# Windowed attention of the odd layer: one pinned plan over 64 head groups, wider value products, the output norm in two steps

## The chip, the cores and the metric

The kernel runs on one core of a Trainium2 chip. The metric is device time in microseconds (us), the median over the runs shown. TensorE is PE in the profile (its weight loads PEld), VectorE is DVE, ScalarE is ACT, GpSimd is POOL, SyncE is SP. Sums are made in one profiled execution.

## The reference, cut to what matters

Two layers over 2048 latent tokens of width 1024 and 256 context tokens. Layer 0 (Fourier mixing beside latent attention) is not touched. Layer 1 is windowed attention with 16 query heads in 4 key/value groups of 4 heads (dimension 64): a block of 128 queries sees the 256 context keys and the three blocks of keys around it, under a mask of +-128 tokens, with one sink logit per head. Its gated output goes through `w_out`, is added to the stream, and a final RMSNorm is stored.

```python
q, k, v, g = split_cols(h_lat @ w_in, ODD_SPLITS)
q, k = apply_rope(q, *rope), apply_rope(k, *rope)
y_l = (windowed_gqa(q, k, v, ck, cv, sink) * silu(g)) @ w_out   # softmax over [ctx, band, sink]
x = x + g_l * y_l
return rmsnorm(x, final_g)
```

## The kernel before, in words

Precision is kept by splitting a float32 operand into a high and a low part; `mm3` (L185 to L188) multiplies two such pairs in three products (high*high, high*low, low*high), so each output product stands under L186, L187 and L188.

**Projection of layer 1** (loop over `seq`, L1688 on). Three passes over the chunks of tokens (1,2,3 / 4,5,6,0 / 7,8), each over five column blocks of `w_in`: 0 and 1 are queries, 2 keys and values, 3 and 4 the gate. In the third pass the order is gate, gate, queries, queries, keys/values (`p2o`). A rotated block is finished in `finish_t` (L1666): VectorE multiplies by the tables, POOL adds, ScalarE rounds the high half, POOL makes the low half; the four stores of the two halves go out one item later (`pend`, `flush`). In the last columns of the third pass the first loads and the row maxima of attention block 0 are mixed in (lists `e6`): all four head groups of block 0, its `chain` and its first `aug`.

**Attention** (L1805 on). 16 query blocks x 4 groups = 64 head groups, each over 4 or 5 key tiles, 312 steps in all. One step (`step6`) is on TensorE a mask product where the tile is at the edge of the band (L1813), two score products of 512 columns (L1814, L1815), then on ScalarE two exponentials (float32 L1819, float16 L1820), and a subtraction that gives the low float16 part (L1821, mostly POOL). `pv` then multiplies probabilities by values: for each of 4 heads a product of 65, of 64 and of 65 columns (L1831 to L1833, the first two with the same weights), into a one-bank accumulator of which there are two. After the last tile of a group VectorE adds the sink term, inverts and scales (L1837 to L1840), and POOL multiplies the gate (L1842).

The exponent is shifted by each row's maximum. `max_band` (L1525 on TensorE, L1529 on VectorE) and `max_ctx` (L1538, L1541) find it from the rounded queries `Q1`; `chain(b)` (L1544 to L1562) joins the maxima of a whole block of 16 heads, splits the result into a high and a low part, and `aug` (L1566 transpose, L1567 copy) puts it into eight extra rows of `Q2`, under the second score product.

Around it: `out_tr` (L1868) transposes the gated rows of the block before into one accumulator bank (`ppo`, one buffer), `split` (L180, L183) writes them to SBUF, `out_mm` multiplies by `w_out` (16 x `mm3`), VectorE and POOL add to the stream (L1882, L1883), and `out_fin` squares, takes the root and scales (L1889 to L1894) and stores. `load_q6` brings the queries of a group in three DMAs (L150). `wload` and `wsplit` bring and split `w_out` during block 0 and 1, through two raw buffers (`wr6`).

What sets the order: a list `plan` per block, with positions as fractions of the block from tables in `TP`. The steps of the next block stand there (`load_q6`, the maxima, `chain` at 0.94, `aug` of its first group at 0.96, the products of the block before). `pv` runs four steps behind the scores. SP's DMAs are kept in program order; TensorE's instructions are not in this part (`pe = nc.tensor` at L1270): the compiler's scheduler may place them otherwise. `pe_ordered` (L152) pins them.

Of the kernel before, what the change touches and what calls it, by code (L numbers as in the profile page):

```python
# [65 lines left out]
class Pool:  # L66
# [36 lines left out]
    'p2o': [3, 4, 0, 1, 2],  # L103
    'b0': {'mx': [0.1, 0.41, 0.59, 0.68], 'mcd': [0.1, 0.26, 0.08, 0.13]},
    'wa': 6,
    'wb': 15,
    'wp': [0.02, 0.0],
    'wd': [0.9, 0.5],
    'we': [0, 0, 0, 0, 0, 0, 0, 0, 0, 0, 0, 0, 0, 0, 0, 1],
    'pps': 3,  # L110
    'ppv': 2,
    'ppo': 1,
    'ppx': 2,
    'pf': 4,
# [27 lines left out]
def tile_hybrid(ctx: ExitStack, tc: tile.TileContext, A, out, dumps=None, stop=99):  # L142
# [1304 lines left out]
    c6, qp6, qs6, sm6, pp6, yp6 = sbuf(), sbuf(), sbuf(), sbuf(2), sbuf(6), sbuf()  # L1447
    wr6 = sbuf(2)
    C6, KL, V1, KV, KK = {}, {}, {}, {}, {}

    def const6():
        C6["mb"] = c6.tile([P, 384], F32, name="mb")
        sp.dma_start(C6["mb"], A["c_band"])
        C6["mask8"] = c6.tile([8, 4, P], F32, name="mask8b")
        sp.dma_start(C6["mask8"], A["c_mask8"])
        sk8 = C6["sk8"] = c6.tile([P, 16], F32, name="sk8")
        sp.dma_start(sk8, A["o_sink"].to_broadcast([P, 16]))
        dve.tensor_scalar(sk8, sk8, 1.0 / GQA_SCALE, None, op0=ALU.mult)
# [16 lines left out]
    def prep_k(t):  # L1475
# [4 lines left out]
        def p0():  # L1480
# [35 lines left out]
    def max_band(b, kv, j):  # L1516
# [3 lines left out]
        if b not in MX:  # L1520
            MX[b] = sm6.tile([P, 2, 16], F32, tag="mx", name=f"mx6_{b}")
# [23 lines left out]
    def chain(b):  # L1545
# [12 lines left out]
        if b:  # L1558
            sink(b)
# [585 lines left out]
```

## Time and profile before

| what | us |
|---|---|
| median of 3 runs | 3030.02 (3030.01 to 3030.97) |
| profiled execution, its own time | 3034.24 |
| its span, first to last instruction | 3032.2 |
| PE busy in the span | 2861.0 (94%) |
| PEld, POOL, DVE, ACT busy | 2299.7, 1632.0, 1462.6, 1427.4 |

Matmuls are pipelined, and a row's duration is longer than the distance to the next start; where a cost of TensorE is wanted, distances between starts are read. The attention of layer 1 begins near 2335 us in the span. PEclk in a table is the granted TensorE clock as a share of 2.4 GHz, averaged over two levels (2.4 and 1.2 GHz).

### The profile page before, as it was taken

The numbers are of one execution on the slowest core, as the hardware profiler recorded it, in microseconds if no ns is written. First come the engines' busy times: TensorE is split into PE (matmuls) and PEld (weight loads), VectorE is DVE, ScalarE is ACT, GpSimd is POOL, SyncE is SP. The second block draws the span as 40 slices with busy tenths as digits, with TensorE's granted clock in tenths as the row PEclk, the third lists the DMA queues.
The fourth block names the chain that finished last, engine by engine and source line by source line (L and its number), as shares of the span: only waits on it lengthen the run. The fifth ranks groups of instructions, "written<-read, shape, count | busy, mean of one in ns | idle before, by whom it ended". The sixth has DMA issues, their size and how long they took to land. (4 is left out here: it accounts for less than half of the span.)

```text
span 3032.2 us, 54284 instructions
## 1 busy us (share of the span) xinstructions
PE 2861.0 (94%) x21388; PEld 2299.7 (76%) x21388; DVE 1462.6 (48%) x2884; ACT 1427.4 (47%) x2131; POOL 1632.0 (54%) x1221
## 2 busy tenths in 40 slices
PE   7999999999999999999999998999997899999998
PEld 4787777877777777777777888989786666677666
DVE  3323315453656665666542234323234666676664
ACT  4333213223577777777773332232222645554554
POOL 2202204035588888888784434353443766766665
PEclk9999999999999999999999998999998999999999
DMA  6453335466310111011016545544464333223321
GB/s 240 153 177 134 130 122 173 142 213 223 104 44 26 44 40 44 26 44 40 26 35 232 188 153 177 187 141 162 152 189 156 105 105 98 84 77 93 102 83 45
DMA packets 299399, 357.13 MB, mean 118 GB/s; under 512 B 40884, under 2 KB 210172, under 8 KB 299144
## 3 DMA queue, kind: packets, MB, share of 16 engines
q1 hardware_dynamic: 231320, 258.73, 27.0%
q10 hardware_dynamic: 67824, 94.93, 8.9%
q8 instruction: 168, 2.75, 0.4%
q14 instruction: 87, 0.71, 0.1%
HBM read 245.82 MB, written 107.76 MB: 117 GB/s over the span
## 5 line engine op out<-in xcount | busy, mean ns | idle before, releaser
L186 PE MATMUL psb<-sbr 128*128 128x512 f32 (+3 forms) x2054 | 744.3, 363 | 14.4 <-ACT sbf L1022 5.7
L188 PE MATMUL psb<-sbr 128*128 128x512 f32 (+3 forms) x2054 | 722.9, 352 | 4.8 <-DVE sbr L183 4.8
L187 PE MATMUL psb<-sbr 128*128 128x512 f32 (+3 forms) x2054 | 723.8, 352 | 2.2 <-POOL sbr L183 2.2
L1188 POOL TENSOR_TENSOR sbf<-sbf 128x1024 f16<-128x1024 f32 (+1 forms) x296 | 624.2, 2112 | 140.8 <-ACT sbf L1187 76.9
L155 PE MATMUL psb<-sbr 100*128 100x512 f32 (+1 forms) x2408 | 624.2, 399 | 21.0 <-DVE sbr L955 14.4
L155 PEld LDWEIGHTS psb<-sbr 100*128 100x128 f32 (+1 forms) x2408 | 425.0, 190 | 112.8 <-issue 17.3
L942 DVE TENSOR_REDUCE sbf<-psb 128x1 f32<-128x512 f32 (+1 forms) x584 | 400.7, 690 | 218.1 <-PE psb L155 203.5
L186 PEld LDWEIGHTS psb<-sbr 128*128 128x128 f32 (+1 forms) x2054 | 390.7, 190 | 81.0 <-issue 12.3
L188 PEld LDWEIGHTS psb<-sbr 128*128 128x128 f32 (+1 forms) x2054 | 390.2, 190 | 63.9 <-DVE sbr L183 6.8
L187 PEld LDWEIGHTS psb<-sbr 128*128 128x128 f32 (+1 forms) x2054 | 390.8, 190 | 53.2 <-POOL sbr L183 3.9
L1821 POOL TENSOR_TENSOR sbf<-sbf 128x512 f16<-128x512 f32 x282 | 338.0, 1213 | 116.0 <-issue 60.1
L1186 ACT ACTIVATE sbf<-psb 128x1024 f32<-128x1024 f32 (+1 forms) x296 | 299.6, 1012 | 200.4 <-PE psb L155 180.5
L183 DVE TENSOR_TENSOR sbr<-sbf,sbr 128x512 fp32r<-128x512 f32 (+3 forms) x212 | 209.1, 1014 | 382.2 <-ACT sbr L180 381.1
L180 ACT CAST sbr<-sbf 128x512 fp32r<-128x512 f32 (+4 forms) x286 | 198.2, 731 | 394.5 <-PE psb L187 149.5
L183 POOL TENSOR_TENSOR sbr<-sbf,sbr 128x512 fp32r<-128x512 f32 (+4 forms) x113 | 166.1, 1482 | 367.9 <-ACT sbr L180 226.3
L1819 ACT ACTIVATE sbf<-psb 128x512 f32<-128x512 f32 x312 | 188.4, 604 | 282.1 <-PE psb L1815 249.8
L1187 ACT ACTIVATE sbf<-psb 128x1024 f16<-128x1024 f32 (+1 forms) x296 | 297.8, 1006 | 0.0
L155 PEld LDWEIGHTS <-sbf 128*128 128x128 f16 x4672 | 213.5, 97 | 72.9 <-issue 65.9
L155 PE MATMUL psb<-sbf 128*128 128x129 f16 (+1 forms) x4672 | 256.8, 207 | 5.2 <-DVE sbf L1214 2.9
L1529 DVE CUSTOM_DVE_ANT_0 sbf<-psb,sbf 128x384 bf16<-128x384 f32 (+1 forms) x256 | 137.8, 538 | 119.4 <-PE psb L1525 108.1
L1820 ACT ACTIVATE sbf<-psb 128x512 f16<-128x512 f32 x312 | 188.2, 603 | 5.5 <-DMA vd<-sbf 5.5
L1831 PEld LDWEIGHTS <-sbf 128*128 128x128 f16 x1248 | 115.5, 97 | 68.3 <-issue 61.8
(259 smaller groups left out, 4303.9 us busy)
## 6 DMA issues: line engine op xcount, KB each, us to landing
sbf<-in_o_w_in_t SPq DMA_DIRECT2D x60, 512.0 KB
sbf<-in_w_in_t SPq DMA_DIRECT2D x54, 512.0 KB
sbf<-in_x SPq DMA_DIRECT2D x32, 512.0 KB
sbf<-in_w_mod SPq DMA_DIRECT2D x32, 512.0 KB
sbr<-q1h SPq DMA_DIRECT2D x128, 128.0 KB
h1d<-sbf ACTq DMA_DIRECT2D x9, 1024.0 KB
sbf<-h1d SPq DMA_DIRECT2D x18, 512.0 KB
x1d<-sbf ACTq DMA_DIRECT2D x16, 512.0 KB
```

The costliest lines, as they stand in the source:

```text
L155: tc.keep_in_program_order(nc.tensor.matmul(*args, **kw))
L180: act.copy(hi, src)
L183: e_lo.tensor_sub(lo, src, hi)
L186: pe.matmul(ps, sh, mh, start=start, stop=False)
L187: pe.matmul(ps, sh, ml, start=False, stop=False)
L188: pe.matmul(ps, sl, mh, start=False, stop=stop)
L942: dve.reduce_max(st["mx"][:, js[0] : js[-1] + 1, c], ps[:, 0 : len(js) * kn].rearrange("p (j k) -> p j k", k=kn), axis=AX.X)
L1186: act.activation(pf[:, :, 0:n], ps[:, :, 0:n], AF.Exp, scale=MLA_SCALE)
L1187: act.activation(ph[:, :, 0:n], ps[:, :, 0:n], AF.Exp, scale=MLA_SCALE)
L1188: pool.tensor_sub(pl[:, :, 0:n], pf[:, :, 0:n], ph[:, :, 0:n])
L1819: act.activation(pf, ps, AF.Exp, scale=GQA_SCALE)
L1821: (dve if (TP["b0"].get("sub", TP["sub"]) if b == 0 else TP["sub"])[kv][n] else pool).tensor_sub(pl, pf, ph)
```

## The change

One plan for all 64 groups with positions counted in steps; TensorE pinned to program order in the attention; steps in pairs (two scores, then two value products six steps behind); the exponent's shift per group instead of per block, in one rounded part; the two products with the same weights joined into one of 129 columns, in an accumulator of two banks, of which there is one; the low part subtracted for two steps at once, on POOL; the output norm split (`out_fin`, `out_end`). In the projection the gate blocks go last in pass three, rotated blocks are rounded and halved one item on and stored one further on, and the gate's stores go out one item on; only two groups of block 0 have their maxima there. `w_out` has three raw buffers.

```diff
-    'p2o': [3, 4, 0, 1, 2],
+    'p2o': [0, 1, 2, 3, 4],
...
-    wr6 = sbuf(2)
+    wr6 = sbuf(3)
...
-    def chain(b):
...
-        dve.tensor_max(m, mx[:, 0, :], mx[:, 1, :])
-        dve.tensor_max(m, m, sk8)
-        dve.tensor_scalar(m, m, -1.0, SHIFT / GQA_SCALE, op0=ALU.mult, op1=ALU.add)
...
-        dve.tensor_copy(m8[:, :, 0, :].bitcast(F32R), m4)
-        dve.tensor_sub(m8[:, :, 1, :].bitcast(F32R), m4, m8[:, :, 0, :])
...
-        pool.tensor_add(es, m, sk8)
...
+    def chain(b, kv):
+
+        m = sm6.tile([P, 4], F32, tag="m", name=f"m6_{b}_{kv}")
+        dve.reduce_max(m, C6["mx", 4 * (b % 2) + kv], axis=AX.X)
+        v = VM[b, kv] = sm6.tile([P, 4], F32, tag="vm", name=f"vm6_{b}_{kv}", bufs=3)
+        act.activation(v.bitcast(F32R), m, AF.Copy, bias=SHIFT / GQA_SCALE, scale=-1.0)
+        es = ES[b, kv] = sm6.tile([P, 4], F32, tag="es", name=f"es6_{b}_{kv}", bufs=4)
+        pool.tensor_add(es, v, C6["sk8"][:, 4 * kv : 4 * kv + 4])
...
-        [lambda: load_q6(0, 0)] + [nop] * 5 + max_all(0),
-        [lambda kv=kv: load_q6(0, kv) for kv in range(1, 4)] + [nop] * 3 + max_all(1) + max_all(2) + max_all(3)
-        + [lambda: chain(0)] + [nop] * 3 + [lambda: aug(0, 0)],
...
+        [nop] * 4 + [const6_end, lambda: load_q6(0, 0)] + [nop] * 4,
+        [nop] * 4 + max_all(0) + [lambda: chain(0, 0)],
+        [lambda: load_q6(0, 1), lambda: load_q6(0, 2), *pk[4]] + [nop] * 4 + max_all(1) + [lambda: chain(0, 1), nop]
+        + [lambda: aug(0, 0)],
...
+        def halve():
+            rh, rl = halves()
             act.copy(rh.bitcast(F32R), r)
             pool.tensor_sub(rl.bitcast(F32R), r, rh)
...
+            pend.append(lambda: store_t(rh, rl, i, rows))
+
+        pend.append(halve)
...
+                flush()
+                pend.append(lambda d=g1d[2 * i + j - 2][:, hf * 512 : (hf + 1) * 512], e=e: act.dma_start(d, e))
...
-    pps, ppv, ppo = psum(TP['pps']), psum(TP['ppv']), psum(TP['ppo'])
+    pe = pe_ordered
+    pps, ppv, ppo = psum(3), psum(1), psum(1)
...
+        if not x:
+            PF["f"] = pp6.tile([P, 2, 512], F32, tag="pf", name=f"pf6_{b}_{kv}_{t}", bufs=2)
...
+        if b == 15 and kv == 3 and n > 1:
+            (pool if x else dve).tensor_sub(pl, pf[:, x], ph)
+        elif x:
+            pool.tensor_sub(PF["l"], pf, PF["h"])
...
+                O[b, kv] = ppv.tile([P, 1024], F32, tag="o", name=f"o6_{b}_{kv}")
...
-                pe.matmul(o, ph[:, js], v[:, kv, 0:65], start=n == 0 and j == 0, stop=False)
-                pe.matmul(o[:, 0:64], ph[:, js], v[:, kv, 65:129], start=False, stop=False)
-                pe.matmul(o, pl[:, js], v[:, kv, 0:65], start=False, stop=last and j == 3)
+                if j % 2 and n:
+                    pe.matmul(o[:, 0:65], pl[:, js], v[:, kv, 0:65], start=False, stop=False)
+                    pe.matmul(o, ph[:, js], v[:, kv, 0:129], start=False, stop=last)
+                else:
+                    pe.matmul(o, ph[:, js], v[:, kv, 0:129], start=n == 0 and j % 2 == 0, stop=False)
+                    pe.matmul(o[:, 0:65], pl[:, js], v[:, kv, 0:65], start=False, stop=last and j % 2 == 1)
...
+                for j in range(4):
+                    dve.scalar_tensor_tensor(t1[:, j], p4[:, j, 65:129], den[:, j], t1[:, j], op0=ALU.mult, op1=ALU.add)
...
-                (dve if b == 15 and kv == 3 else pool).tensor_mul(g, g, t1)
...
+                pool.tensor_mul(g, g, t1)
...
-        dve.tensor_scalar(v, ss, 1.0 / D, EPS, op0=ALU.mult, op1=ALU.add)
+        act.activation(v, ss, AF.Copy, bias=EPS, scale=1.0 / D)
         rsqrt(y, v)
-        dve.scalar_tensor_tensor(x, x, y, C6["fgb"], op0=ALU.mult, op1=ALU.mult)
+        pool.tensor_mul(x, x, C6["fgb"])
+        YS[b] = x, y
+
+    def out_end(b):
+        x, y = YS.pop(b)
+        act.mul(x, x, y)
         sp.dma_start(out[b * P : (b + 1) * P, :], x)
...
+    for u, (b, kv) in enumerate(groups):
+        if u > 2:
+            at(start[u - 5] + 0.3 if u > 5 else -1, lambda b=b, kv=kv: load_q6(b, kv))
+        if u > 1:
+            s0 = start[u] - 9
+            for j in range(4):
+                at(s0 + 0.8 * j, lambda b=b, kv=kv, j=j: max_band(b, kv, j))
+            for jj in range(2):
+                at(s0 + 3.2 + 0.8 * jj, lambda b=b, kv=kv, jj=jj: max_ctx(b, kv, jj))
+            at(s0 + 4.1, lambda b=b, kv=kv: (chain(b, kv), sink(b, kv)))
+        if u:
+            at(start[u] - 2.2, lambda b=b, kv=kv: aug(b, kv))
+    for x in range(TP["wa"], 17):
+        w0 = 1.5 * (x - TP["wa"] - 1) if x > TP["wa"] else -1
...
+        t0, t1, m0, md = (8.2, 10.2, 13.8, 0.85) if b < 13 else (8.2, 10.2, 12.8, 0.42) if b == 13 else (3, 6, 6.5, 0.42)
+        at(s1 + t0, lambda b=b: out_tr(b, 0))
+        at(s1 + t1, lambda b=b: out_tr(b, 1))
+        at(s1 + m0, lambda b=b: out_load(b))
+        for i in range(16):
+            at(s1 + m0 + md * i, lambda b=b, i=i: out_mm(b, i // 8, i % 8))
+        at(s1 + m0 + md * 16 + 0.6, lambda b=b: out_fin(b))
+        at(s1 + m0 + md * 16 + (4.5 if b < 14 else 1.0), lambda b=b: out_end(b))
...
+                turn = g % 2 == 0 and len(pvq) > 5 and pvq[0][1]
+                if turn:
+                    pvq.pop(0)[0]()
+                    late = 1
+                step6(b, kv, n, t, nts[b], g % 2)
+                g += 1
+                run(min(g - 0.5, S[15] + 14.9))
+                if g % 2 == 0:
+                    run_pv((6 if b < 15 else 4) + late)
+                    late = 0
+                    run(min(g, S[15] + 14.9))
```

## Rows read from the trace of the kernel before

**Rows 1.** Windows: busy us (count) of PE, PEld, DVE, ACT, POOL; clock, DMA, GB/s.
```profile
2282.00:2335.00 53.00, 42.25 (x315) 41.89 (x316) 27.22 (x67) 9.95 (x17) 20.67 (x21) 0.87 0.46 146
2335.00:2384.50 49.50, 33.11 (x278) 22.79 (x276) 26.42 (x65) 26.13 (x50) 36.84 (x35) 0.76 0.48 149
2432.70:2947.50 514.80, 476.28 (x4562) 357.05 (x4560) 342.58 (x828) 277.53 (x542) 336.80 (x313) 0.99 0.31 89
```

**Rows 2.** Waits of PE, 2384.5 to 2947.5: total us, times, longest.
```profile
PE psb L1525 <- DMA sbr<-q1l: 14.2, 8, 2.2
PE psb L1566 <- DVE sbf L1555: 9.7, 13, 0.8
PE psb L1868 <- DVE sby L183: 8.7, 13, 0.7
PE psb L1525 <- DMA sbr<-q1h: 5.3, 4, 1.9
```

**Rows 3.** Waits of SP's queue, 2370 to 3010: total us, times, longest.
```profile
SPq L150 <- DVE sbf L1894: 356.4, 14, 25.6
```

**Rows 4.** Timeline of PE in block 1: start, duration, line, shape, idle before.
```profile
2417.62 0.48 PE L1814 MATMUL psb<-sbr 128*128 128x512 f32 x1
2417.94 0.40 PE L1815 MATMUL psb<-sbr 72*128 72x512 f32 x1
2418.18 0.21 PE L1831 MATMUL psb<-sbf 128*128 128x65 f16 x1
...
2418.56 0.38 PE L1813 MATMUL psb<-sbf 128*128 128x512 bf16 x1
...
2419.00 0.39 PE L1815 MATMUL psb<-sbr 72*128 72x512 f32 x1
2420.13 0.27 PE L1566 MATMUL psb<-sbf 128*8 128x128 f32 x1 [0.74 <-DVE sbf L1555]
```

**Rows 5.** Timeline of PE at the end of block 1.
```profile
2428.89 0.19 PE L1833 MATMUL psb<-sbf 128*128 128x65 f16 x1
2429.75 0.66 PE L1868 MATMUL psb<-sbf 128*128 128x128 f32 x4 [0.67 <-DVE sby L183]
...
2435.21 0.58 PE L1525 MATMUL psb<-sbr 128*128 128x384 f32 x2 [2.21 <-DMA sbr<-q1l]
```

**Rows 6.** Windows of two whole blocks, columns as in rows 1.
```profile
2564.40:2608.27 43.87, 40.27 (x380) 30.64 (x380) 28.58 (x69) 22.84 (x46) 27.80 (x26) 0.96 0.34 89
2649.97:2692.33 42.36, 39.29 (x381) 29.24 (x380) 28.55 (x69) 23.15 (x46) 28.06 (x27) 1.00 0.31 93
```

**Rows 7.** Timeline of PE in layer 0's attention: 16 products, 8 of 129 columns, 8 of 65.
```profile
1004.69 0.87 PE L155 MATMUL psb<-sbf 128*128 128x129 f16 x16
1005.36 2.10 PE L155 MATMUL psb<-sbr 100*128 100x512 f32 x8
```

**Rows 8.** Waits of PE, 2282 to 2384.5.
```profile
PE psb L1525 <- DMA sbr<-q1l: 12.6, 4, 6.2
PE psb L1525 <- DVE sbf L1529: 7.8, 2, 7.4
```

**Rows 9.** The page's group of POOL's pair subtraction in layer 0's attention.
```profile
L1188 POOL TENSOR_TENSOR sbf<-sbf 128x1024 f16<-128x1024 f32 (+1 forms) x296 | 624.2, 2112 | 140.8 <-ACT sbf L1187 76.9
```

**Rows 10.** Groups of POOL and DVE, 2334 to 3032: busy us, mean ns | idle before.
```profile
L1821 POOL TENSOR_TENSOR sbf<-sbf 128x512 f16<-128x512 f32 x282 | 338.0, 1213 | 116.0 <-issue 60.1 <-ACT sbf L1820 37.1 <-POOL sbf L1821 12.2
L1842 POOL TENSOR_TENSOR sbf<-sbf 128x256 f32<-128x256 f32 x63 | 52.0, 825 | 103.1 <-DVE sbf L1840 91.4 <-PE psb L1538 11.7
L1883 POOL TENSOR_TENSOR sbf<-sbf 128x512 f32<-128x512 f32 x30 | 38.5, 1282 | 2.1 <-DVE sbf L1882 1.6
L183 POOL TENSOR_TENSOR sbr<-sbf,sbr 128x512 fp32r<-128x512 f32 x10 | 13.2, 1317 | 3.1 <-ACT sbr L180 3.0
L1840 DVE TENSOR_TENSOR sbf<-psb,sbf 128x256 f32<-128x256 f32 x64 | 27.1, 424 | 2.3
L1837 DVE TENSOR_TENSOR sbf<-psb,sbf 128x4 f32<-128x4 f32 x64 | 10.2, 160 | 9.8 <-PE psb L1833 8.0
```

More of the change, by code (lines that the diff above doesn't have):

```diff
@@ L1657, in flush @@
     def flush():
-        while pend:
+        for _ in range(len(pend)):
             pend.pop(0)()
@@ L1668, in finish_t, with halves @@
         pv = ps.rearrange("p (f t) -> p f t", f=2)
[L1669 to L1670 removed]
+        def halves():
+            return [ep5.tile([P, 2, 256], F32, tag=t, name=f"{t}5_{n}_{i}", bufs=2) for t in ("rh", "rl")]
         if i:
@@ L1900, in tail_tr @@
     def tail_tr(q, k0, n):
+        if not q:
+            YT[15] = (
+                yp6.tile([P, KT, P], F32R, tag="yh", name="yh6_15"),
+                yp6.tile([P, KT, P], F32R, tag="yl", name="yl6_15"),
+            )
         yh, yl = YT[15]
@@ L1952, in tail_end, with tiles_of, at @@
             (sp if hf else act).dma_start(out[15 * P : 16 * P, hsl], x[:, hsl])
-    parity = 0
-    for b in range(16 - TP["nb"], 16):
+    def tiles_of(b):
+        lo, hi = band(b)
+        return [0, 1] + [2 + i for i in range(lo, hi + 1)]
+    nts = [len(tiles_of(b)) for b in range(16)]
+    S = [4 * sum(nts[:b]) for b in range(17)]
+    groups = [(b, kv) for b in range(16) for kv in range(4)]
+    start = [S[b] + kv * nts[b] for b, kv in groups]
+    plan = []
+    def at(pos, f):
+        plan.append((pos, len(plan), f))
@@ L1956, in tile_hybrid, with g_load @@
+    def g_load(b):
         G[b] = yp6.tile([P, D], F32, tag="g", name=f"g6_{b}", bufs=2)
         sp.dma_start(G[b], g1d[b])
[L1958 to L1978 removed]
@@ L1995, in tile_hybrid @@
-        if b == 15:
-            at(TP["z"][11], lambda: out_fin(14))
-            for kv in range(1, 4):
-                at(TP["z"][11 + kv], lambda kv=kv: aug(15, kv))
-        elif b:
-            at(T["ofin"], lambda: out_fin(b - 1))
-        if b < 15:
-            for f in prep_k(b + 5):
-                at(0.1, f)
-            for kv in range(4):
-                at(T["ql"][kv], lambda kv=kv: load_q6(b + 1, kv))
-                m0 = T["mx"][kv]
-                for j in range(4):
-                    at(m0 + T["mxd"][kv] * j / 4, lambda kv=kv, j=j: max_band(b + 1, kv, j))
-                for jj in range(2):
-                    at(T["mc"][kv] + T["mcd"][kv] * jj, lambda kv=kv, jj=jj: max_ctx(b + 1, kv, jj))
-            at(T["ch"], lambda: chain(b + 1))
-            at(T["aug0"], lambda: aug(b + 1, 0))
@@ new lines, in tile_hybrid, with run, run_pv @@
+    at(S[15] + 14.5, lambda: out_load(15))
+    at(S[15] + 13.4, lambda: tail_tr(0, 0, 4))
+    for i in range(8):
+        at(S[15] + 15 + 0.1 * i, lambda i=i: tail_mm(i // 2, i % 2))
+    plan.sort(key=lambda z: z[:2])
+    def run(pos):
+        while plan and plan[0][0] < pos:
+            plan.pop(0)[2]()
+    def run_pv(keep):
+        while len(pvq) > keep:
+            pvq.pop(0)[0]()
+    run(0)
+    g = late = 0
+    for b in range(16):
+        for kv in range(4):
+            for n, t in enumerate(tiles_of(b)):
+                turn = g % 2 == 0 and len(pvq) > 5 and pvq[0][1]
+                if turn:
+                    pvq.pop(0)[0]()
+                    late = 1
[6 more added lines that the diff above has]
+                    run(min(g, S[15] + 14.9))
@@ L2035, in tile_hybrid @@
+    tail_tr(1, 4, 2)
+    run(S[15] + 15.45)
+    run_pv(2)
+    run(S[16])
+    tail_mm(4, 0)
+    run_pv(0)
+    tail_mm(4, 1)
+    tail_mm(5, 0)
+    tail_mm(5, 1)
+    tail_tr(2, 6, 2)
     tail_end()
```

226 lines of the change are left out of this document (68 added, 158 removed).

## The prediction

> **What bounds the kernel now.** I read the windows first. In the long stretch of like blocks, 2432.7 to 2947.5, PE is busy 476.3 of 514.8 us at a clock of 0.99, POOL 336.8, DVE 342.6, ACT 277.5 [rows 1]: TensorE bounds it, and what an edit is worth is the TensorE time that it frees. Before that stretch lies the join of projection and attention, 2282 to 2384.5: 102.5 us of which PE is busy 75.4, at clocks of 0.87 and 0.76 [rows 1]; there other things bound.
>
> Then the waits of PE in the blocks [rows 2]. Three stand out, each about once per block: `max_band` for query loads (14.2 + 5.3 us), `aug` for the `chain` (9.7), and the second `out_tr` for the halving of the first (8.7). The queue of SP says where the loads were: 356.4 us in 14 waits for L1894, the last step of the output norm [rows 3]. The store stands in SP's order ahead of the next block's loads. The timelines show the size of each: L1815 at 2419.00 to L1566 at 2420.13 is 1.13 us where the same product is followed after 0.24 at 2417.94 to 2418.18 [rows 4]; L1833 to L1868 takes 0.86 [rows 5] where products of that width are about 0.03 apart (twelve in 0.38, 2418.18 to 2418.56 [rows 4]). The wait for the load there is 2.21 [rows 5].
>
> **The change part by part.**
>
> *Query loads.* `load_q6` issues three DMAs on SP. They now come five groups ahead of their group's scores and about 16 steps (some 30 us at 42.36 us per 20 steps [rows 6]) ahead of its maxima, so a store that holds SP for some us delays nothing that PE needs. The store itself (`out_end`) stands 3.9 steps behind `out_fin`, and the next `out_load`, which needs the same buffer, 1.9 steps behind the store. Gain: 14.2 + 5.3 = 19.5 us [rows 2].
>
> *Shift per group.* `chain` for four heads stands 2.7 steps ahead of its `aug`, with two scores, value products and products of `w_out` between. Per block five DVE operations go; four reductions, four small ScalarE operations and three more POOL additions come, on engines that are busy under 70% [rows 1]; priced at nothing, bounds 0 to 1 us per block if DVE were to hold PE. Gain: 13 x (1.13 - 0.24) = 11.6 us [rows 4]. The transpose narrows from eight to four columns and the score's extra rows from 8 to 4: nothing.
>
> *Transposes two steps apart.* The second `out_tr` comes two steps, some 3.8 us, after the first. Gain: 13 x (0.86 - 0.03) = 10.8 us [rows 5].
>
> *Clock.* Of ten like blocks from 2476 to 2905 four have a clock of 0.96; one such has PE busy 40.27 where one at 1.00 has 39.29 [rows 6]. They follow the longest load waits. Gain: 4 x 0.98 = 3.9.
>
> *Value products.* Twelve per step take 0.38 us [rows 4]. Eight of 129 and 65 columns take half of 1005.36 - 1004.69 = 0.67, that is 0.335 [rows 7]. Gain: 312 x 0.045 = 14.0 us; bounds 0 and 20. The Trainium skill, "TensorE: Matmul & The Clock Gate", Back-to-back issue gap, speaks against the wide one: in a real kernel some 81 ns per product of 128 columns. By it the change would lose some 22 us here instead (an estimate from that page: 312 x 4 x 0.029 us, less the gain of 14). The trace disagrees: a wide and a narrow product together take 0.67 / 8 = 0.084 us [rows 7].
>
> *Pairs.* The first float32 product after a run of float16 ones costs extra: L1814 to L1815 takes 0.32 instead of 0.24 [rows 4]; with a mask between, 2418.56 to 2419.00 for 512 + 512 columns, nothing. 192 of 312 steps have no mask. Now there is one run per two steps, and 28 more by `turn`: 184 for 312. Gain: 192 x (1 - 184/312) x 0.08 = 6.3.
>
> *Join.* Waits for loads and for VectorE there are 20.4 us [rows 8], and 0.13 x 2 x 53.0 + 0.24 x 2 x 49.5 = 38 us ran at the lower clock level [rows 1]. The queries' blocks of the last pass now come first, and only two of four groups have their maxima before the attention, with loads a whole block of columns ahead. For the projection's last 53.0 us I take 40: 42.25 busy, less a part of the 6.9 us that the clock would give back. For block 0 POOL decides: eight pair subtractions at 2.11 [rows 9], ten splits of `w_out` at 1.32, four gates at 0.83 [rows 10] and about 1 us of small ones, 34.4; with 2 us of waits 36.4 for 49.5. Gain 13 + 13 = 26 us; bounds 0 (another late load takes the place of these) and 33. `wsplit`'s loads pass `load_q6(1,2)` on SP; its maxima come 13 steps later.
>
> *Halving one item on, gate stores one on.* ScalarE's rounding, POOL's low half and four stores per item move. PE works on six accumulators there and waited for none of it in [rows 8]: nothing, bounds 3 us either way (one load wait of rows 8).
>
> *One accumulator of two banks.* The first value product of a group now waits for VectorE's drain of the group before: 0.16, a reciprocal like it, 0.42, and four new operations of 64 columns. By 0.42 for 256 and 0.16 for 4 columns [rows 10] one is 0.22; together 1.6 us. In the plan two scores, a mask, two row maxima and two `mm3` stand between, some 2.9 us at 0.24 per 512 columns [rows 4]; where no `mm3` do, some 1.5. Bounds 0 and 63 x 1.66 = 105 us. I take the lower end, since the cover is counted in the same rows, and 9 us for this, the two `out_tr` and the two halves of `out_mm`, which share one bank, together (0.6 per block).
>
> *Output norm.* POOL takes the 1024-column multiply (two of 1.28 [rows 10], 2.6), ScalarE the scaling; off PE. POOL per block: 10 x 2.11 + 4 x 0.83 + 2 x 1.28 + 2.6 + 0.8 = 30.4 of some 38 us; with 2 x 1.213 [rows 10] per pair, 33.6.
>
> *Tail.* The last drain is 4 x 0.22 longer and its gate is on POOL (0.83 for 0.42): 1.3 us, on the path.
>
> Sum: 19.5 + 11.6 + 10.8 + 3.9 + 14.0 + 6.3 + 26 - 9 - 1.3 = 81.8. The profiled execution took 3034.2, 4.2 above the median of the runs; 3034.2 - 81.8 - 4.2 = **2948 us**.
>
> **The rivals.**
>
> *The accumulator decides (slower).* The drain comes late, since VectorE works in its own order and row maxima may stand ahead; POOL's wait for L1840, 91.4 us in all [rows 10], shows that the drain does come late. If each of 63 hand-overs shows its whole 1.66 us: 2948 + 105 = 3053. It decides from 82 / 63 = 1.3 us per hand-over. Against: the cover above. 8%.
>
> *POOL becomes the bound.* 33.6 per block, and 4 x 1.45 us of waits for the drain as now (91.4 / 63), is 39.4; with `out_fin`'s two steps waiting in its queue 40.5. My block is 42.36 [rows 6] less 1.5, 0.89, 0.83, 0.9 and 0.5 (loads, `aug`, transposes, value products, pairs) and with 0.6 of new waits, 38.3. 14 x 2.2 = 31, 2979 us. 12%.
>
> *The join keeps its length.* TensorE waits in its pinned order for `load_q6(0,3)`, or stays at 1.2 GHz in a block 0 that POOL leaves it idle in: no 26 us, 2974. 16%.
>
> *All cover holds.* A block is TensorE's products alone: 40 scores and 48 of `w_out` at 0.24, eight masks at 0.2, twenty steps at 0.335, row maxima 4.8 (10,240 columns at the same rate), transposes and changes of type some 2.2, 36.4 for 38.3: 14 x 1.9 = 27 off, 2921. 18%.
>
> *It does not take effect*: the scheduler's order had these waits hidden from the end already. Against: PE itself waited [rows 2]. 4%, no change.
>
> **How the numbers follow.** The forecast has 42% (2935 to 2962). Faster: 42 + 18 + 16 + 12 = 88%; same 4%; slower 8%, with 0.2% (6 us) as what a measurement of this kernel can tell from no change. The range runs from below the fourth rival, 2915, to 3000, beyond POOL as the bound with part of the join lost; it leaves out the first rival and the no-change case.
>
> **What would show it.** Right: blocks of 37 to 39 us with no wait of L1566, L1868 or L1525 over 0.3 us; eight value products in 0.34; SP's wait for the norm without PE waiting behind it; block 0 about 36 us with POOL near full. Wrong: waits of the first value product for L1840 or its four successors (accumulator), of ScalarE for POOL's subtraction (POOL), a clock under 0.8 in block 0 (join).

## The result, and the profile after

The changed kernel takes 3063.63 us (median of 6 runs, 3055.54 to 3076.32) where the kernel before took 3030.02: a ratio of 1.0114, 95% interval 1.0097 to 1.0131, some 34 us slower. 2948 us was forecast, with 3000 as the upper end. The profiled execution took 3056.98 us, its span is 3055.2 (before: 3034.24 and 3032.2). Three of the six runs lie at 3055.5 to 3057.0 us and three at 3070.3 to 3076.3 with a lower granted clock (0.958 to 0.961 for 0.970 to 0.975); the profile is of one of the first three, so it shows 23 us of the 34.

In the profile after, pinned products stand under L124, pinned transposes under L128, the projection's `mm3` under L155 to L157, SP's DMAs under L119. `split` is L149 (ScalarE, rounding) and L152 (low half). L1502 reduces `max_band`, L1514 `max_ctx`; L1523 rounds the shift, L1528 is the sink's exponential. L1802 and L1803 are the two exponentials, L1807 the pair subtraction, L1826 to L1831 the drain, L1833 the gate, L1874 and L1875 the end of `out_mm`. Of the output norm L1881 is the square, L1886 POOL's multiplication, L160 the root, L1891 the scaling.

Where the time lies is told by the first float16 exponential of each block (the timeline of ScalarE, L1820 before, L1803 after); a stretch reaches from one to the next, in us:

| stretch | before | after | run e1 | run f2 | run i3 |
|---|---|---|---|---|---|
| start to block 0 | 2351.7 | 2349.2 | 2346.6 | 2329.8 | 2335.2 |
| of it from the second pass's end on | 140.3 | 137.7 | 139.0 | 127.3 | 128.5 |
| block 0 | 33.1 | 33.1 | 32.9 | 30.3 | 30.3 |
| block 1 | 37.7 | 38.9 | 39.1 | 38.5 | 36.0 |
| one of blocks 2 to 13, mean | 42.9 | 42.5 | 38.4 | 38.4 | 38.1 |
| block 14 | 40.8 | 49.9 | 43.9 | 43.9 | 43.4 |
| block 15, to the last exponential | 37.2 | 45.5 | 45.3 | 39.1 | 37.6 |
| from there to the end | 16.9 | 28.2 | 27.4 | 24.0 | 24.1 |

The second pass's end is the start of its last gate's activation on ScalarE (L1785 before, L1762 after): 2211.4, 2211.5, 2207.6, 2202.5 and 2206.6 us. The changed kernel and its variants below have the same program up to there, and the kernel before alone took from 3022.8 to 3040.4 us in 19 runs beside e1; so what differs ahead of that mark is put down to the run and not to an edit, and the second row leaves it out.

So the like blocks gain 0.4 us each where 4 had been forecast, the join gains 2.5 in all where 26 had, and 28.7 us are lost from block 14 on (9.1 + 8.3 + 11.3).

The windows, columns as in [rows 1]: a piece of the projection's last pass, the stretch of like blocks, and the end.

```profile
2245.00:2272.00 27.00, 14.64 (x81) 13.10 (x80) 8.89 (x15) 6.50 (x18) 9.28 (x11) 0.68 0.60 186
2432.70:2947.50 514.80, 462.17 (x3623) 367.63 (x3634) 311.40 (x971) 303.80 (x653) 364.84 (x267) 0.96 0.28 88
2947.50:3055.00 107.50, 79.02 (x535) 61.41 (x536) 41.37 (x129) 43.45 (x90) 54.33 (x42) 0.86 0.12 43
```

PE is busy 462.2 of 514.8 us where it was 476.3 [rows 1], at a clock of 0.96 for 0.99: it waits more, although there is less work (37.1 us per block in e1, below, for 39.3 in [rows 6]). PE's waits in the like blocks, 2400 to 2950 (total, times, longest), answer to [rows 2]:

```profile
PE psb L128 <- DVE sby L152: 34.1, 12, 2.9
PE psb L128 <- DVE sbf L1502: 10.9, 13, 1.1
PE psb L124 <- DVE sbf L1502: 4.9, 14, 0.4
PE psb L128 <- ACT sbf L1803: 3.9, 13, 0.3
```

The waits for query loads are gone. The wait of the second `out_tr` for the halving of the first, 8.7 us before [rows 2], is 34.1. ScalarE's waits in the same stretch name what stands ahead of it:

```profile
ACT sbf L1881 <- POOL sbf L1875: 45.9, 13, 3.5
```

One block's timeline, all engines:

```profile
2477.36 0.61 ACT L1803 ACTIVATE sbf<-psb 128x512 f16<-128x512 f32 x1
...
2478.10 2.14 POOL L1807 TENSOR_TENSOR sbf<-sbf 128x1024 f16<-128x1024 f32 x1 [1.48 <-issue]
...
2478.60 0.60 PE L128 MATMUL psb<-sbf 128*128 128x128 f32 x4
...
2480.21 1.26 POOL L1875 TENSOR_TENSOR sbf<-sbf 128x512 f32<-128x512 f32 x1
...
2481.50 1.06 ACT L1881 ACTIVATE sbf<-sbf 128x1024 bf16<-128x1024 f32 x1 [3.53 <-POOL sbf L1875]
...
2483.60 0.59 ACT L149 CAST sby<-psb 128x512 fp32r<-128x512 f32 x1
...
2484.22 0.69 DVE L152 TENSOR_TENSOR sby<-psb,sby 128x512 fp32r<-128x512 f32 x1 [3.18 <-ACT sby L149]
...
2484.83 0.15 DVE L1826 TENSOR_TENSOR sbf<-psb,sbf 128x4 f32<-128x4 f32 x1
...
2484.97 1.11 PE L128 MATMUL psb<-sbf 128*128 128x128 f32 x4 [2.84 <-DVE sby L152]
```

Read it backwards. The second transposes (2484.97, the second `out_tr`) wait for the low half of the first (2484.22), since both use one bank, and that for ScalarE's rounding (2483.60). What it rounds was there from 2479.20 on, but ScalarE stood at the square for the norm of the block before, 3.53 us, for POOL's residual addition (2480.21), which POOL had put behind a pair subtraction of 2.14 us. The drain of the accumulator (2484.83) stood behind the low half on VectorE, too. The Trainium skill, "PSUM — Partial Sum Buffer", Engine vs sequencer instructions, has ScalarE's, VectorE's and GpSimd's queues as strictly first in, first out; the trace agrees, with ScalarE idle for 3.53 us while a rounding it could have done stood behind the square.

At the end the same square and scaling stand ahead of the last exponentials (timeline of the tail):

```profile
3021.42 1.06 ACT L1881 ACTIVATE sbf<-sbf 128x1024 bf16<-128x1024 f32 x1 [1.88 <-POOL sbf L1875]
...
3023.66 1.87 DVE L1805 TENSOR_TENSOR sbf<-sbf 128x512 f16<-128x512 f32 x1 [3.40 <-ACT sbf L1803]
...
3025.97 1.15 ACT L1891 ACTIVATE sbf<-sbf 128x1024 f32<-128x1024 f32 x1 [1.86 <-POOL sbf L160]
...
3028.79 0.72 POOL L1833 TENSOR_TENSOR sbf<-sbf 128x256 f32<-128x256 f32 x1
3029.57 0.69 PE L128 MATMUL psb<-sbf 128*128 128x128 f32 x2 [8.12 <-POOL sbf L1833]
```

In the projection's last pass the waits for query loads and row maxima of [rows 8] are replaced by one for rounded weights (waits of PE, 2202 to 2349):

```profile
PE psb L155 <- ACT sbr L149: 15.3, 4, 6.5
PE psb L1498 <- DVE sbf L1502: 3.8, 1, 3.8
```

### The profile page after: what moved, and what is told of

It is laid out like the page before. It is cut to its first block, busy times and chain, and to the rows that moved or that the text cites. A ratio compares the mean times of both kernels' runs of the same rounds, so it can differ in the third digit from the quotient of the medians.

```text
span 3055.2 us, 51991 instructions
## 1 busy us (share of the span) xinstructions
PE 2850.6 (93%) x20122; PEld 2317.0 (76%) x20140; DVE 1422.0 (47%) x3064; ACT 1466.4 (48%) x2285; POOL 1664.9 (54%) x1159
## 5 line engine op out<-in xcount | busy, mean ns | idle before, releaser
L124 PE MATMUL psb<-sbr 96*128 96x512 f32 (+6 forms) x3492 | 949.5, 401 | 34.3 <-DVE sbr L924 14.4
L155 PE MATMUL psb<-sbr 128*128 128x512 f32 (+3 forms) x2054 | 744.9, 363 | 25.5 <-ACT sbr L149 15.3
L124 PEld LDWEIGHTS psb<-sbr 96*128 96x128 f32 (+3 forms) x3492 | 629.9, 194 | 170.1 <-issue 20.6
L157 PE MATMUL psb<-sbr 128*128 128x512 f32 (+3 forms) x2054 | 723.2, 352 | 2.2 <-DVE sbr L152 2.1
L155 PEld LDWEIGHTS psb<-sbr 128*128 128x128 f32 (+1 forms) x2054 | 390.7, 190 | 93.7 <-ACT sbr L149 17.6
L124 PE MATMUL psb<-sbf 128*128 128x129 f16 (+2 forms) x7270 | 441.4, 212 | 12.5 <-DVE sbf L1831 4.3
L157 PEld LDWEIGHTS psb<-sbr 128*128 128x128 f32 (+1 forms) x2054 | 390.2, 190 | 61.1 <-DVE sbr L152 4.6
L124 PEld LDWEIGHTS <-sbf 128*128 128x128 f16 (+1 forms) x7288 | 344.8, 99 | 120.1 <-issue 102.0
L1807 POOL TENSOR_TENSOR sbf<-sbf 128x1024 f16<-128x1024 f32 x155 | 332.0, 2142 | 171.1 <-ACT sbf L1803 68.6
L149 ACT CAST sbr<-sbf 128x512 fp32r<-128x512 f32 (+4 forms) x286 | 198.4, 732 | 392.0 <-PE psb L156 152.8
L152 DVE TENSOR_TENSOR sbr<-sbf,sbr 128x512 fp32r<-128x512 f32 (+3 forms) x212 | 208.1, 1010 | 380.5 <-ACT sbr L149 379.0
L152 POOL TENSOR_TENSOR sbr<-sbf,sbr 128x512 fp32r<-128x512 f32 (+4 forms) x113 | 165.2, 1476 | 363.9 <-ACT sbr L149 219.8
L1802 ACT ACTIVATE sbf<-psb 128x512 f32<-128x512 f32 x312 | 187.3, 600 | 118.9 <-PE psb L124 116.9
L124 PE MATMUL psb<-sbr,sby 128*128 128x512 f32 (+1 forms) x740 | 228.8, 415 | 1.3 <-DVE sby L152 0.5
L1803 ACT ACTIVATE sbf<-psb 128x512 f16<-128x512 f32 x312 | 187.0, 599 | 0.1
L1502 DVE CUSTOM_DVE_ANT_0 sbf<-psb,sbf 128x384 bf16<-128x384 f32 (+1 forms) x256 | 137.7, 538 | 83.7 <-PE psb L124 53.7
```

Of the source, the lines that this page charges most:

```text
L124: tc.keep_in_program_order(nc.tensor.matmul(*args, **kw))
L149: act.copy(hi, src)
L152: e_lo.tensor_sub(lo, src, hi)
L155: pe.matmul(ps, sh, mh, start=start, stop=False)
L157: pe.matmul(ps, sl, mh, start=False, stop=stop)
L1802: act.activation(pf[:, x], ps, AF.Exp, scale=GQA_SCALE)
```

## The experiments

Each is a change of the changed kernel; ratios are to the kernel before on the same chip.

**e1: the squares behind both roundings.** The scheduler orders ScalarE; the plan pins TensorE and SP alone. So the edit moves and pins. The next load of the residual and the end of the norm move with the squares.

```diff
-        at(s1 + m0, lambda b=b: out_load(b))
+        at(s1 + m0 + (1.6 if b < 14 else 0), lambda b=b: out_load(b))
-        at(s1 + m0 + md * 16 + 0.6, lambda b=b: out_fin(b))
+        at(s1 + m0 + md * 16 + (3.0 if b < 13 else 0.6), lambda b=b: out_fin(b))
-        at(s1 + m0 + md * 16 + (4.5 if b < 14 else 1.0), lambda b=b: out_end(b))
+        at(s1 + m0 + md * 16 + (6.9 if b < 13 else 4.5 if b < 14 else 1.0), lambda b=b: out_end(b))
-        act.activation(jk, x, AF.Square, accum_out=ss)
+        tc.keep_in_program_order(act.activation(jk, x, AF.Square, accum_out=ss))
```

> The changed kernel with one thing moved: for blocks 0 to 12 the squares of the output norm (out_fin) stand 2.4 steps later and are pinned behind the roundings of both out_tr; out_end and the next out_load move with them. Theory Q (ScalarE's queue): the squares wait for POOL's second residual addition (45.9 us in 13 waits), the rounding of the first out_tr waits behind them, VectorE's low half behind that, and the second out_tr, which needs the same bank, behind that. Then PE's 34.1 us in 12 waits for the low half go, and with them some 12 half-clock stretches of 3.4 us (1.7 us each): 45 to 58 us faster than the changed kernel, 3000 to 3015, blocks of 38 to 39 us. Theory T (two steps are too few for one bank, whatever ScalarE's order): the wait for the low half stays above 1.5 us per block, gain under 20 us. Rival A of the prediction (the accumulator decides): nothing changes by over 5 us, the first value products of a group wait.

Measured: 3002.32 us, ratio 0.9902 (0.9876 to 0.9929); every block from 2 to 13 takes 38.4. A block's window, and PE's waits from 2400 to 2930:

```profile
2457.00:2495.40 38.40, 37.08 (x302) 29.26 (x301) 25.66 (x81) 24.94 (x56) 30.14 (x23) 1.00 0.34 104
```

```profile
PE psb L124 <- DVE sbf L1502: 8.8, 27, 0.4
PE psb L128 <- DVE sbf L1502: 4.9, 14, 0.4
PE psb L128 <- ACT sbf L1803: 3.9, 13, 0.3
PE psb L124 <- DVE sbf L1874: 0.3, 1, 0.3
PE psb L124 <- DVE sbf L1831: 0.2, 1, 0.2
```

The wait for L152 is gone altogether, the clock is 1.00, and the accumulator (L1831) is waited for once, 0.2 us. Theory Q holds; T and A fall. From the second pass's end to the end of the span e1 takes 788.4 us for 843.7, that is 55 us less; by the medians it is 61.

**g1: the same places without the pin.** e1 less its last change:

```diff
-        tc.keep_in_program_order(act.activation(jk, x, AF.Square, accum_out=ss))
+        act.activation(jk, x, AF.Square, accum_out=ss)
```

> The run e1 without the pin: the squares stand 2.4 steps later in the plan, but nothing holds them there on ScalarE, whose order the scheduler chooses. If the place in the plan were enough, the time is e1's (3002). If the scheduler puts the squares ahead of the roundings again, PE's waits for the low half and ScalarE's waits for POOL's addition stay (over 25 and over 35 us) and the time is that of the changed kernel, 3050 to 3075.

Measured: 3048.84, ratio 1.0055 (1.0039 to 1.0072), with these waits of PE and of ScalarE in the stretch of e1:

```profile
PE psb L128 <- DVE sby L152: 32.9, 12, 2.8
```

```profile
ACT sbf L1881 <- POOL sbf L1875: 42.4, 12, 3.5
```

A place in the plan is not a place in ScalarE's queue. (The time lies just below the range given; the waits are as expected.) The pin without the move is in e3, below, where blocks 0 to 12 keep their places and every square is pinned; there these waits of PE are left, 2400 to 2910:

```profile
PE psb L128 <- DVE sby L152: 24.5, 12, 2.9
```

So it takes both.

**e2: the second `out_tr` later, the squares left.**

```diff
-        at(s1 + t1, lambda b=b: out_tr(b, 1))
+        at(s1 + t1 + (2 if b < 13 else 0), lambda b=b: out_tr(b, 1))
```

> The changed kernel with the second out_tr of blocks 0 to 12 two steps later (12.2 for 10.2), the squares left where they are. Theory Q: ScalarE still waits some 3.5 us for POOL's addition in each block, but the bank is free when the second transposes come: PE's wait for the low half falls from 34 to under 6 us; some of it returns as scores or value products that wait for late exponentials, so 20 to 45 us faster, and ScalarE's wait at the squares stays at 40 us or more. Theory T: the whole 45 to 58 us come back here and not in the run before. Rival A: no change.

Measured: 3071.96, ratio 1.0133 (1.0107 to 1.016): nothing came back, against both theories' numbers, and a like block takes 44.0 us for 42.5. PE's waits from 2400 to 2930 begin:

```profile
PE psb L124 <- DVE sbf L1514: 14.6, 12, 1.2
PE psb L124 <- ACT sbf L1803: 10.9, 7, 1.7
PE psb L124 <- DMA sbr<-q1h: 7.9, 5, 1.6
```

The second transposes no longer wait, but ScalarE still stands 42.4 us at the squares, and now products wait for late exponentials, reductions and loads; the clock over 2432.7 to 2947.5 is 0.90. Whoever moves the victim leaves the stall.

**e3: the norm of blocks 13 and 14 late**; squares and scalings of all blocks pinned (as in e1, and `act.mul` likewise), and the last two residual loads later (neither is shown).

```diff
-        at(s1 + m0 + md * 16 + 0.6, lambda b=b: out_fin(b))
-        at(s1 + m0 + md * 16 + (4.5 if b < 14 else 1.0), lambda b=b: out_end(b))
+        at(s1 + m0 + md * 16 + (0.6 if b < 13 else 2.6 if b < 14 else 2.2), lambda b=b: out_fin(b))
+        at(s1 + m0 + md * 16 + (4.5 if b < 13 else 7.4 if b < 14 else 2.6), lambda b=b: out_end(b))
```

> The changed kernel with the output norm of blocks 13 and 14 alone later and pinned on ScalarE (out_fin of 13 two steps, of 14 behind the last scores; out_end and the loads of the residual move with them). From the first exponential of block 14 to the end the changed kernel takes 123.6 us, the kernel before 94.9. Theory Q: most of these 28.7 us are exponentials and roundings that stand behind squares and scalings that wait for POOL: 14 to 22 us faster, the 8.1 us wait of the tail's second transposes under 4. Rival (the tail's own serial work: a longer drain and the gate on POOL): under 4 us.

Measured: 3031.78, ratio 1.0004 (0.9984 to 1.0024). From block 14 to the end 113.3 us (46.2 + 39.2 + 27.9) for 123.6: 10.3 faster, less than expected; the tail's wait for the gate falls from 8.12 to 3.23 us. The rest of the gain lies in the blocks before, 40.8 us instead of 42.5 in most of them: the pin of the squares holds in all blocks, so this run is not the ending alone.

**f1: e1 and e3 together, the tail's second transposes behind its first eight products.**

The end positions of block 14 lie 0.6 to 0.8 steps behind e3's, and the last residual has a buffer of its own (not shown).

```diff
...
-    tail_tr(1, 4, 2)
     run(S[15] + 15.45)
     run_pv(2)
-    run(S[16])
+    run(S[15] + 15.8)
+    tail_tr(1, 4, 2)
+    run(S[16] + 1)
```

> The changed kernel with the output norm of every block behind its neighbours' roundings: squares pinned and moved as in the run e1 for blocks 0 to 12, two steps later for 13, behind the last scores for 14 (with a buffer of its own for the last residual), and the tail's second transposes behind its first eight products. Theory Q: e1's profile ends at 2996.0 with 43.9, 45.3 and 27.4 us for block 14, block 15 and what follows the last exponential; e3 had 46.2 and 39.2 for the two blocks. Here block 14 takes 39 to 41, block 15 38 to 40, the rest 21 to 25: 2973 to 2988. Rival (the ending is long because a half block of products of w_out lies later than before): block 14 and the rest stay above 43 and 26, 2988 or more.

Measured: 2991.13, ratio 0.9861 (0.9841 to 0.9881); block 14 43.9, block 15 39.3, then 24.0. Of block 14 the rival was right (of what follows the last exponential, 24.0 and not 26, it was not): block 14 has 24 products of `w_out` more than a like block (the second half of block 12's beside all of block 13's), 24 x 0.24 = 5.8, and is 5.5 longer. The work was moved there from block 1, which has 24 products fewer, but block 1 does not give the time back: it takes 38.5 us, at a clock of 0.88 for 1.00 in a like block.

```profile
2379.30:2417.80 38.50, 35.59 (x281) 27.72 (x281) 26.87 (x83) 22.83 (x51) 29.32 (x22) 0.88 0.42 126
```

**e4 and f3: the old order of the last pass.** e4 has the first change alone, f3 is f1 with both:

```diff
-    'p2o': [0, 1, 2, 3, 4],
+    'p2o': [3, 4, 0, 1, 2],
...
-        pend.append(halve)
+        halve() if n == 14 else pend.append(halve)
```

> The changed kernel with the order of the last projection pass as before (3, 4, 0, 1, 2), all else as changed. Theory S: in the new order the attention's first key loads, the weight loads and the rotated blocks' stores share the same 40 us, the weights come late (PE waits 15.3 us for their rounding in 4 waits, and the clock is 0.68 over 2245 to 2272); with the old order these waits go and the first exponential comes 10 to 20 us earlier than 2349. Rival (the join keeps its length): the waits for late loads and row maxima that the kernel before has in its last block come back (20 us), the first exponential comes within 4 us of 2349.

> The run f1 with the old order of the last projection pass and, in its last block alone, the rotated blocks halved at once instead of one item on. In e4 the projection's last product comes about 2316 and PE then waits 8.4 and 9.6 us for exponentials and the first aug, while ScalarE's queue holds the last halving and its stores, which wait for POOL. Theory H (the delayed halving stands in ScalarE's queue ahead of the attention's first steps): these waits fall under 6 us together, the first exponential comes at 2318 to 2328, and f3 is 25 to 35 us faster than f1. Rival (the join keeps its length: another load or the first splits of w_out hold it): the first exponential stays at 2332 or later.

Measured: e4 3041.85, ratio 1.0062 (1.0032 to 1.0092), first exponential at 2335.9, 13.3 earlier, of which 7.3 behind the second pass's end (130.4 us for 137.7). No wait for rounded weights is left there, which is theory S's sign, at less than its size; but in their place PE waits 9.6 us for an exponential and 8.4 for the first shift, so the rival is right in part. f3 2977.39, ratio 0.9818 (0.9802 to 0.9834), first exponential at 2342.9, 131.5 behind the second pass's end; theory H falls, since these waits of PE, 2310 to 2390, are as long as e4's:

```profile
PE psb L124 <- ACT sbf L1803: 12.0, 4, 9.0
PE psb L128 <- ACT sbf L1523: 8.9, 1, 8.9
```

In f3's timeline the last rotation on POOL begins at 2330.67, behind six splits of `w_out` there, and ScalarE's rounding (2332.10) waits for it. That this is the cause was not tried.

**f2: f1 with the attention's key and value loads two projection blocks later**, beside the gates:

```diff
-        [const6, nop, *pk[0], nop, *pk[1], nop, *pk[2], nop, *pk[3]],
-        [nop] * 4 + [const6_end, lambda: load_q6(0, 0)] + [nop] * 4,
-        [nop] * 4 + max_all(0) + [lambda: chain(0, 0)],
-        [lambda: load_q6(0, 1), lambda: load_q6(0, 2), *pk[4]] + [nop] * 4 + max_all(1) + [lambda: chain(0, 1), nop]
-        + [lambda: aug(0, 0)],
+        [const6] + [nop] * 9,
+        [nop] * 4 + [const6_end] + [nop] * 5,
+        [lambda: load_q6(0, 0), *pk[0], nop, *pk[1], nop, *pk[2], nop, *pk[3]],
+        [lambda: load_q6(0, 1), lambda: load_q6(0, 2), *pk[4]] + max_all(0) + [lambda: chain(0, 0)] + max_all(1)
+        + [lambda: chain(0, 1), nop] + [lambda: aug(0, 0)],
```

> The run f1 with the attention's first key and value loads two projection blocks later (beside the gates, behind the rotated blocks' stores) and the row maxima of the first two groups in the last projection block. Theory S (key loads, weight loads and the rotated blocks' stores collide on the DMA queues): PE's waits for rounded weights (15.3 us in 4 in the changed kernel) fall under 4 us, the 17 us at the lower clock go, 12 to 22 us faster than f1. Rival (the join keeps its length): the keys then come late for the row maxima or the second aug, and f2 is within 5 us of f1.

Measured: 2971.83, ratio 0.9801 (0.9784 to 0.9819), 19 us below f1; the first exponential comes at 2329.8 for 2348.3. Of these 18.5 us 11.3 lie behind the second pass's end (127.3 for 138.6) and are the edit's; the other 7.2 lie ahead of it, in code that f1 and f2 share. PE's wait for rounded weights, 2202 to 2349, and the window 2245 to 2272 again:

```profile
PE psb L155 <- ACT sbr L149: 2.5, 1, 2.5
```

```profile
2245.00:2272.00 27.00, 26.11 (x183) 24.90 (x183) 12.75 (x18) 8.24 (x19) 10.82 (x11) 0.84 0.54 185
```

Theory S holds: the loads beside the rotated blocks' stores made the weights late. Which resource they share there (SP's order or the DMA engines) was not separated.

**i1: the first sinks' exponentials behind the first scores** and pinned there (not shown), and block 14's second transposes and products of `w_out` later, all on top of f2:

```diff
-    at(-1, lambda: (sink(0, 0), sink(0, 1)))
+    at(0.6, lambda: (sink(0, 0), sink(0, 1)))
...
-else (3, 6, 6.5, 0.42)
+else (3, 7.2, 7.3, 0.4)
```

> The run f2 with the exponentials of the first two sinks pinned behind the first two scores, and the second transposes of block 14 with its products of w_out 0.8 to 1.2 steps later. In f2 five loads of an activation table of 1.28 us each stand between 2318 and 2329 on ScalarE, where these exponentials alternate with the last gates' activation, and PE waits 5.2 us for the first exponentials. If the table loads are that wait: only one of them is left there, the first exponential comes 4 to 6 us earlier; with the 4.1 us wait of block 14 gone, 6 to 11 us faster than f2 (2961 to 2966). Rival (the first exponentials wait for the last gate anyway): under 3 us from the join.

Measured: 2971.8, ratio 0.9789 (0.9768 to 0.981), no different from f2. Of the five table loads one is left, yet PE still waits for the first exponentials (5.5 us in 4). Behind the second pass's end the first exponential comes after 123.6 us (125.9 in i2, which has the same start) for 127.3 in f2 (127.2 to 128.5 in i3, i4 and j1, which have f2's): 1 to 5 us earlier, where 4 to 6 were expected and under 3 by the rival. Whether the table loads were the limit stays open; the medians cannot show so little. Block 14's transposes and products stand in block 15's stretch, which takes 39.6 us for f2's 39.1: no gain.

**i2: i1 with `aug` one step earlier.**

```diff
-            at(start[u] - 2.2, lambda b=b, kv=kv: aug(b, kv))
+            at(start[u] - 3.2, lambda b=b, kv=kv: aug(b, kv))
```

> The run i1 with every aug one step earlier, so that it no longer stands between two row maxima of the same two banks. In f2 each block still has 0.5 to 0.6 us waits of aug and of the row maxima beside it, about 2.1 us per block. If they are for the banks that VectorE drains: 1 to 1.5 us per block less, 14 to 20 us faster than i1. Rival (the shift's own chain is then late, or VectorE is busy with something else): no gain, aug waits for ScalarE's rounding of the shift.

Measured: 3001.79, ratio 0.9894 (0.9872 to 0.9916), 30 us slower than i1. PE's waits from 2437 to 2821:

```profile
PE psb L128 <- ACT sbf L1523: 15.6, 18, 1.8
PE psb L124 <- DVE sbr L1535: 5.1, 9, 0.6
```

The waits for the row maxima's banks are gone, and `aug` waits for ScalarE's rounding of the shift (L1523) instead: the rival.

**i4: f2 with the two `out_tr` next to each other.**

```diff
-        t0, t1, m0, md = (8.2, 10.2, 13.8, 0.85) if b < 13
+        t0, t1, m0, md = (10.1, 10.2, 13.8, 0.85) if b < 13
```

> The run f2 with the two out_tr of blocks 0 to 12 next to each other again (10.1 and 10.2). By the prediction's term the second then waits 0.83 us per block for the halving of the first: 8 to 14 us slower than f2. With ScalarE busy with two exponentials in front of the rounding it is up to 2 us per block: up to 28 us slower. Rival (the distance is worth nothing once the squares are out of the way): within 4 us of f2.

Measured: 3009.16, ratio 0.9918 (0.99 to 0.9935); a block takes 41.1 for 38.4, and i4 is 34 us slower than f2 from the second pass's end on, more than the 28 expected at most. PE, 2437 to 2821:

```profile
PE psb L128 <- DVE sby L152: 17.2, 9, 1.9
```

**i3: f2 with the value products of before; j1: i3 with four extra operations in the drain.**

```diff
-                if j % 2 and n:
...
+                pe.matmul(o[:, 0:65], ph[:, js], v[:, kv, 0:65], start=n == 0 and j % 2 == 0, stop=False)
+                pe.matmul(o[:, 0:64], ph[:, js], v[:, kv, 65:129], start=False, stop=False)
+                pe.matmul(o[:, 0:65], pl[:, js], v[:, kv, 0:65], start=False, stop=last and j % 2 == 1)
...
-                for j in range(4):
-                    dve.scalar_tensor_tensor(t1[:, j], p4[:, j, 65:129], den[:, j], t1[:, j], op0=ALU.mult, op1=ALU.add)
```

In j1 the loop over `j` stays, with `p4[:, j, 0:64], 0.0` for `p4[:, j, 65:129], den[:, j]`: zero times the accumulator.

> The run f2 with the value products of the kernel before (65, 64 and 65 columns per head; the drain's four extra operations go with them), all else as in f2. By the prediction's term, 0.045 us per step in 312 steps, the wide products are worth 14.0 us: f2 plus 10 to 16 us. Rival (in f2 the products' time lies beside other limits): within 4 us of f2.

> The run i3 (narrow value products) with four VectorE operations of 64 columns per group put back into the drain; they add zero times the accumulator, so the result is the same. i3's steady block takes 38.1 us, f2's 38.4, though f2's wide products take 0.68 us less per block by their own rows (20 steps x 0.034). Theory V (the four operations on VectorE give that back, since row maxima then leave their two banks later): a steady block of 38.7 to 39.3 us here, 8 to 17 us slower than i3. Rival W (the four operations are covered, and the wide products lose the time elsewhere, in the scores or row maxima that follow them): within 0.2 us per block of i3, 38.0 to 38.3.

Measured: i3 2965.72, ratio 0.9771 (0.9751 to 0.979); j1 2978.73, ratio 0.9824 (0.9805 to 0.9842). A like block takes 38.1 in i3, 38.6 to 38.7 in j1, 38.4 in f2. VectorE's group in f2 (2437 to 2821, ten blocks) and the windows of i3 and of j1:

```profile
L1831 DVE SCALAR_TENSOR_TENSOR sbf<-psb,sbf 128x64 f32<-128x64 f32 x160 | 34.2, 276 | 0.7
```

```profile
2437.00:2821.00 384.00, 376.78 (x3833) 301.51 (x3830) 230.97 (x646) 247.31 (x543) 304.22 (x223) 1.00 0.33 101
```

```profile
2437.00:2821.00 384.00, 373.73 (x3787) 297.23 (x3784) 245.82 (x796) 249.40 (x540) 299.01 (x219) 1.00 0.32 98
```

Four small operations per group on an engine that is busy 231 of 384 us make a block 0.6 us longer: theory V, at the lower end of its range. Part of it shows as waits of `aug` for a bank that a row maximum holds, 2437 to 2821, in i3 and in j1:

```profile
PE psb L128 <- DVE sbf L1502: 0.2, 1, 0.2
```

```profile
PE psb L128 <- DVE sbf L1502: 3.6, 10, 0.4
```

i3 is the fastest kernel here, 2.3% faster than the one before; against f2, both expectations for it fail. From the first exponential to the end it takes 628.3 us and f2 636.7, so the wide products with their longer drain cost 8 us instead of gaining 14; 2.5 of the 8 lie in block 1, which has a clock of 0.97 in i3 and of 0.88 in f2.

## Why the prediction was wrong

**The step that failed** is "Transposes two steps apart": "The second `out_tr` comes two steps, some 3.8 us, after the first. Gain: 13 x (0.86 - 0.03) = 10.8 us". The distance was right (2478.60 to 2482.13, where PE begins to wait); what was missed is ScalarE's queue between them. The plan itself had put the square there: `out_fin` of a block stands 13.8 + 13.6 + 0.6 = 28.0 steps behind the start of the next, which is step 8.0 of the block after that, and the first `out_tr` stands at its step 8.2. In place of the gain 34.1 us of waits came, with the clock that fell after them. e1 took both away, 61 us by the medians (3063.6 to 3002.3). Its block of 38.4 meets the forecast block of 38.3 in part by luck: the value products gave none of their 0.9 and new waits took 1.3 where 0.6 had been given; what made up for that was not found. In the new plan, with that queue clear, the distance is worth 41.1 - 38.4 = 2.7 us per block (i4), where the kernel before waited 0.83. "Output norm ... off PE" failed with it: off PE, but ahead of what PE waits for.

**Join.** 26 us forecast, 2.5 measured. The lower bound named ("another late load takes the place of these") is what happened, with the weights as the late load. f2 gains 140.3 - 127.3 = 13.0 up to the first exponential, the 13 that were forecast for the projection, and 2.8 in block 0. The other 13, "for block 0 POOL decides", could not come: the 49.5 us that it set against POOL's 36.4 begin at the first score (2335.02), but the first float16 exponential comes at 2351.68, and from there block 0 took 33.1 before the change.

**Tail.** 1.3 us forecast, 28.7 lost from block 14 on. f1 takes 16.5 of it back (107.1 for 123.6): norm and gate in ScalarE's and POOL's queues. Of the 12.2 left in f1 against the kernel before, 7.1 lie behind the last exponential: the last block's first 24 products of `w_out`, 5.8 us at 0.24, ran ahead of it before (3007.68 to 3013.97, the exponential at 3015.34) and behind it in f1 (2961.05 to 2967.48, the exponential at 2961.62). Block 15 is 2.1 longer all the same; PE waits in it 3.9 us for the gate ahead of block 14's second transposes and 1.6 for the drain of the accumulator. Block 14, with its 24 products more, is 3.1 longer. What each of these is worth by itself was not tried.

**Value products.** The rows were right: two steps' 16 products take 0.676 us in e1's blocks (mean distance to the next product), 0.338 per step for 0.335 forecast and 0.38 before; a wide and a narrow one together take 0.084 as in [rows 7]. The Trainium skill, "TensorE: Matmul & The Clock Gate", Back-to-back issue gap, has some 81 ns for each product of 128 columns, and here 84 ns hold two. The gain of 14 us is still not there: f2 is no faster than i3. The drain's four operations, priced as covered in "One accumulator of two banks", cost 0.6 us per block (j1 to i3), and the wide products give back 0.2 to 0.3 (j1 to f2).

**Shift per group.** The waits for the chain are gone (9.7 us in [rows 2]), but 17.6 us of waits for banks and ScalarE took their place in e1's blocks (8.8 + 4.9 + 3.9, 13.8 blocks): "0 to 1 us per block if DVE were to hold PE" was the right mechanism, at the upper end of its range (13.7 us in 13.8 blocks) where nothing had been charged.

**Right.** Query loads: SP still waits for the scaling (100.5 us in 13), and in the like blocks of the changed kernel no product waits for a load. Halving one item on: nothing, from the projection's first gate to the second pass's end it takes 235.9 us for 236.7. The accumulator: 9 us given for it and the other shared bank, 0.2 measured for it in e1's like blocks; the slower rival had the right sign and the wrong place. POOL as the bound: 364.8 of 514.8 us, no; what hurt was the order of its queue. The change in pairs was not tried by itself.

f2, the change with three placements mended, is at 2972 for a forecast of 2948. From the second pass's end on its profile gains 820.8 - 764.0 = 56.8 us where the terms add up to 81.8: 15.8 for 26 in the join and block 0, 53.1 in blocks 1 to 13, and a loss of 12.1 from block 14 on; the terms for the blocks were 57.1, and the tail's was a loss of 1.3.

## What to carry to other kernels

When one engine's order is pinned, ask of every other engine what its in-order queue holds ahead of the short operation that frees a bank, above all an instruction that waits for a slow engine; move that one and pin it there, not its victim. A distance between two uses of one bank is only worth what the queues of its release chain leave of it. Operations added to an engine that is busy 60% of the time are not free if a bank is released behind them. And measure what an edit gives from a mark in code that it cannot touch: these variants differ by up to 11 us at the projection's first gate already (1967.0 in f2, 1978.0 in f3), more than most terms here are worth.

## What was not expected of the hardware

The clock made each wait dearer: with 12 waits of about 2.8 us in 515 us the granted clock of the stretch was 0.96, with waits of at most 0.4 us it was 1.00 (e1), and between the changed kernel and e1 4 us per block went for 2.8 us of waiting. Behind the wait above the granted clock was 0.50 from 2485 to 2488, the lower level, and four transposes took 1.11 us for 0.60 ahead of it. Three loads of an activation table, 1.28 us each, stand at the join after (f2 has five) where the last gates' activation and the sinks' exponentials alternate; with one left (i1) the time did not change clear of noise.
